# Two mixer layers: 22 of 62 convolution taps leave VectorE for ScalarE and GpSimd, small sums and weight splits come to it

## The chip, the cores and the metric

One core of a Trainium2 chip runs the kernel. The metric is the device time of one execution in microseconds. TensorE (PE) multiplies matrices, VectorE (DVE), ScalarE (ACT) and GpSimd (POOL) work on tiles of 128 partitions, and SyncE (SP) issues the loads. Each engine takes its instructions in a fixed order; semaphores hold one until the data and the buffers that it needs are there.

## The reference, cut to what matters

A first block of two layers, each `token_mixers` and `conv_ffn`, is followed by a second block of two layers that the change does not touch. The mixers of one layer (sequence 512, width 1024):

```python
def token_mixers(h, ...):
    proj = h @ w_in                                   # 512 x 1024 @ 1024 x D_IN, cut into 13 parts
    y_a = sc_b * depthwise_conv(sc_c * sc_h, w_sc_conv)          # 3 taps, 256 channels
    o_f = gla_scan(q, k, v, la_f, True)                          # linear attention, 4 heads, forward
    o_b = flip(gla_scan(flip(q), flip(k), flip(v), flip(la_b), False))   # and backward
    y_b = rms_norm(o_f + o_b, g_gla_head) * silu(gg)
    q_c = concat([qm[..., :64], apply_rope(qm[..., 64:])])       # 4 heads, 64 + 32 wide
    k_c = concat([kvm[..., :64], broadcast(apply_rope(kr))])
    y_c = blocked_attention(q_c, k_c, v_c, 96 ** -0.5)           # full softmax, 4 heads x 4 blocks
    u = depthwise_conv(a * sigmoid(gate), w_cfm_dw)              # 31 taps, 256 channels
    y_d = silu(layer_norm(u, g_cfm_ln, b_cfm_ln))
    y = concat([rms_norm(yb, gb) for yb, gb in zip((y_a, y_b, y_c, y_d), gains)])
    return y @ w_out
```

## The kernel before, in words

Activations lie feature-major, as tiles of 128 channels by 512 positions. A product of fp32 quality is made as three matmuls of reduced precision (`mm3`, lines 368 to 370): every operand is split into a rounded part `hi` (a ScalarE cast, line 374) and the rest `lo` (a subtraction, line 376). The weights stream from HBM in units of 128x1024 (`raw`) and are split on arrival. Most units have their `lo` made by VectorE; in the mixers `st.slow` (line 672) gives six units of a layer to GpSimd.

In `mixers_` four generators are written as if side by side, and `merge` (lines 237 to 249) lets that one go on which is furthest behind its share: `linear` (the linear attention), `mla` (softmax attention, 16 heads-by-blocks, each scores, softmax, transposes, values), `convolutions` (all the projections, then the two convolutions, then the first half of the output product) and `output` (the second half). This sets the program order. The tile framework then places each engine's instructions in a queue by its own simulated times (`schedule_with_timeline_sim=True`), keeping to what depends on what and to the buffers: a tile's name has a fixed number of buffers, and a new tile waits until the oldest one's last reader is done.

`convolutions` is the generator that the prediction follows. `projections` multiplies the last weights and makes the 3-tap branch `ya` (the last step is line 760). Then come `ya`'s squares (line 579), their sums over channels by 16 matmuls with one column (`feat_r`, line 562), and `ya`'s split into `g` for the output product (`put`, lines 890 and 891). The 31-tap convolution runs over two channel groups: 31 VectorE instructions each, all into `cacc` (lines 783 and 784). Its mean over channels comes from matmuls with ones (line 792), then follow the subtraction (795), squares, `feat_rsqrt`, gain, bias and the silu (801 to 806), `put`, and last `out_part` for the branches 0 and 3, whose first matmul is the first `L368 AP<-hi,g` of a layer's mixers. No output product stands ahead of it in TensorE's queue. The second half of the output product, the layer norm and the feed-forward part follow.

The lane `C` has four buffers named `Cw` of 128x512, shared by the projections' temporaries, `ya`, the squares and the tanh of the branch. `rsqrt` of up to 4 columns is a VectorE scale and a GpSimd power (lines 383 and 384). `feat_rsqrt` builds a diagonal matrix by VectorE (line 573) for each of 4 blocks and multiplies it by ones. The linear attention's running sums (lines 956 to 968) and the head mask (line 1008) are GpSimd's, and so are the 4 copies of the turned keys (line 1082). Each head's query is turned by three VectorE instructions of 32 partitions (lines 1073 to 1075).

Of the kernel before, what the change touches and what calls it, by code (L numbers as in the profile page):

```python
# [11 lines left out]
F32 = mybir.dt.float32  # L12
# [9 lines left out]
S = 512  # L22
# [12 lines left out]
SLOTS = 96  # L35

# [32 lines left out]
def layout(i):  # L69
# [11 lines left out]
    for l in range(2):  # L81
# [18 lines left out]
        q = []  # L100
        for h in range(4):
            r = rng(96 * h + 64, 32)
            q += rng(96 * h, 64) + r + r[16:] + r[:16]
# [156 lines left out]
class Lane:  # L260
# [23 lines left out]

    def d(self):
        return self.tile((128, 128), F32, "d", 2)


class Net:
# [351 lines left out]
    def block1_consts(self):  # L641
        self.gmask = self.blk.tile([128, 8, 128], U8, name="gmask")
        self.trig = self.blk.tile([128, S], F32, name="trig1")
        self.hmask = self.const("hmask", 256, self.blk)
# [5 lines left out]
    def mixers_(self, l, x):  # L650
# [7 lines left out]
        LN = Lane(self, "N", w=3)  # L658
# [13 lines left out]
        st.slow = (2, *range(6, 20, 3))  # L672
# [23 lines left out]
        with self.tc.issue_after(last.ins):  # L696
            if l == 0:
                raw = self.rawp.tile([128, 1024], F32, tag="raw", name=self.nm("raw"))
                nc.sync.dma_start(raw, self.A["gmask"])
                nc.gpsimd.tensor_copy(self.gmask.rearrange("p a b -> p (a b)"), raw)  # L700
                self.angles(M, "pos", 0, 1, 2, self.trig)
            tmp = M.w()
            ve.tensor_tensor(out=tmp[64:96], in0=kr[96:128], in1=self.trig[96:128], op=OP.mult)
            ve.tensor_tensor(out=kr[64:96], in0=kr[64:96], in1=self.trig[64:96], op=OP.mult)
            ve.tensor_tensor(out=kr[64:96], in0=kr[64:96], in1=tmp[64:96], op=OP.add)
# [65 lines left out]
        def convolutions():  # L771
# [122 lines left out]
    def gla_scores(self, L, q, k, dec):  # L894
# [41 lines left out]
        while m < 128:  # L936
# [19 lines left out]
            po.tensor_tensor(out=nf[:, :, 1], in0=fp[:, :, 1], in1=bc(ftl), op=OP.add)  # L956
            ac.copy(nf[:, :, 0], fp[:, :, 0])
            po.tensor_tensor(out=nb[:, :, 0], in0=bs[:, :, 0], in1=bc(btr), op=OP.add)
            ac.copy(nb[:, :, 1], bs[:, :, 1])
            if m == 1:  # L960
                po.tensor_copy(ns[:, :, 0], ftr)
                po.memset(ns[:, :, 1], 0.0)
                po.tensor_copy(np_[:, :, 1], btl)
                po.memset(np_[:, :, 0], 0.0)
            else:
                po.tensor_tensor(out=ns[:, :, 0], in0=fs[:, :, 0], in1=bc(ftr), op=OP.add)
                ac.copy(ns[:, :, 1], fs[:, :, 1])
                po.tensor_tensor(out=np_[:, :, 1], in0=bp[:, :, 1], in1=bc(btl), op=OP.add)
                ac.copy(np_[:, :, 0], bp[:, :, 0])
# [18 lines left out]
    def gla_states(self, L, inter, ends, gv):  # L988
# [4 lines left out]
        for d, order in enumerate(((0, 1, 2), (3, 2, 1))):  # L993
# [51 lines left out]
    def mla(self, L, wm, cq, ckv, kr, g_q, g_kv, attended):  # L1045
# [20 lines left out]
        def queries(h):  # L1066
            ps = L.P()
            for k in range(2):
                o = (2 * h + k) * 128
                nc.tensor.matmul(ps, wm[:, 0, o:o + 128], cq[k], start=k == 0, stop=k == 1)  # L1070
            ac.copy(Q[0:64, h], ps[0:64])
            tmp = L.w()
            ve.tensor_tensor(out=Q[64:96, h], in0=ps[64:96], in1=T[64:96], op=OP.mult)
            ve.tensor_tensor(out=tmp[64:96], in0=ps[96:128], in1=T[96:128], op=OP.mult)
            ve.tensor_tensor(out=Q[64:96, h], in0=Q[64:96, h], in1=tmp[64:96], op=OP.add)

        def keys(h):
            ps = L.P()
            nc.tensor.matmul(ps, wm[:, 1, h * 64:h * 64 + 128], ckv, start=True, stop=True)
            for j in range(2):  # L1080
                ac.copy(K[0:64, h + j], ps[64 * j:64 * j + 64])
                nc.gpsimd.tensor_copy(K[64:96, h + j], kr[64:96])
# [4 lines left out]
        for h in range(4):  # L1087
            queries(h)
            yield 1.7
# [969 lines left out]
```

## Time and profile before

| | |
|---|---|
| median of 3 runs | 3015.38 us (3015.05 to 3016.5) |
| the profiled execution, its own time | 3014.35 us |
| its span | 3012.6 us |
| busy in the span: PE / DVE / ACT / POOL | 95% / 72% / 48% / 15% |
| DVE instructions, POOL instructions | 3477, 443 |

The profiled execution lies 1.0 us under the median. A row of the profile gives line, engine, operation, names written and read (buffer numbers left out), shape and count, then busy time and the mean of one. An entry in brackets at the end of a timeline's row is the idle time of that engine before it and what ended it. Times of the timeline run from the span's start. "L784" is line 784 of the kernel before; the changed kernel's lines stand 3 to 4 lower up to line 600 and 10 to 20 higher from line 784 on.

### The profile page before, as it was taken

Reading aid. Unit: us, or ns where it says so; the run is one execution under the profiler, and the core shown is the slowest. Engines: PE = TensorE matmul, PEld = TensorE weight load, DVE = VectorE, ACT = ScalarE, POOL = GpSimd, SP = SyncE. Lnnn points to the kernel's source line nnn. Section 1 sums busy time; section 2 is a strip of 40 time slices with the busy share of each in tenths; the row PEclk is TensorE's granted clock in tenths of the full one; section 3 lists DMA queues with packets and bytes.
Section 4 is the critical chain, followed back from the end, with each engine's and each line's share of the span. In section 5 each row is a group of like instructions: output and inputs, shape, how many; then the busy total and the mean of one; then the engine's idle time right before and its main releaser. Section 6 shows DMA issues by size and latency. Waiting matters only on the chain.

```text
span 3012.6 us, 38089 instructions
## 1 busy us (share of the span) xinstructions
PE 2869.8 (95%) x14030; PEld 2250.3 (75%) x14030; DVE 2174.2 (72%) x3477; ACT 1434.1 (48%) x2214; POOL 456.2 (15%) x443
## 2 busy tenths in 40 slices
PE   7999999999999999999999998999799999979995
PEld 6777888888678888878777775776587877857773
DVE  6998655666968555687965467999678764579996
ACT  4444432324444333345444325887345444248883
POOL 3412000013111000012001021110311010022103
PEclk9999999999999999999999998999799999989998
DMA  5121332342213322352222377995631322669983
GB/s 191 35 106 49 99 98 92 99 143 70 64 54 95 98 98 98 106 170 89 78 88 84 105 264 266 379 389 223 230 109 60 95 88 80 245 224 374 384 321 135
DMA packets 128655, 457.35 MB, mean 152 GB/s; under 512 B 15761, under 2 KB 16977, under 8 KB 127057
## 3 DMA queue, kind: packets, MB, share of 16 engines
q1 hardware_dynamic: 117840, 425.50, 40.2%
q0 software_dynamic: 7168, 16.79, 1.8%
q10 hardware_dynamic: 3456, 12.58, 1.0%
q8 instruction: 112, 1.84, 0.2%
q14 instruction: 79, 0.64, 0.1%
HBM read 429.12 MB, written 27.26 MB: 151 GB/s over the span
## 4 chain that ended last, share of the span: by engine, by line
PE 64%; DVE 7%; ACT 2%; DMA 2%; issue 1%; POOL 1%; POOLq 0%; SPq 0%; DVEq 0%; ACTq 0%; another core or an unknown queue 0%
PE AP L368 12%; PE AP L369 12%; PE AP L370 12%; PE HP L368 4%; PE HP L369 4%; PE HP L370 4%; PE YP L369 2%; PE YP L370 2%; PE YP L368 2%; PE BP L369 1%; PE BP L370 1%; PE BP L368 1%; DVE cacc L784 1%; DVE lo L376 1%; PE O L1569 1%
## 5 line engine op out<-in xcount | busy, mean ns | idle before, releaser
L368 PE MATMUL AP<-g,hi 128*128 128x512 f32 (+1 forms) x1888 | 728.2, 387 | 25.3 <-ACT wide L445 7.4
L369 PE MATMUL AP<-g,hi 128*128 128x512 f32 (+1 forms) x1888 | 721.9, 383 | 8.2 <-DVE g L376 8.2
L370 PE MATMUL AP<-g,lo 128*128 128x512 f32 (+1 forms) x1888 | 723.0, 383 | 0.0
L376 DVE TENSOR_TENSOR lo<-raw,hi 128x1024 fp32r<-128x1024 f32 x322 | 409.6, 1274 | 371.4 <-ACT hi L374 362.2
L374 ACT CAST hi<-raw 128x1024 fp32r<-128x1024 f32 x334 | 350.1, 1051 | 581.9 <-PE AP L369 386.4
L368 PEld LDWEIGHTS AP<-g,hi 128*128 128x128 f32 x1888 | 360.3, 191 | 97.2 <-ACT wide L445 7.6
L369 PEld LDWEIGHTS AP<-g,hi 128*128 128x128 f32 x1888 | 360.4, 191 | 75.6 <-DVE g L376 9.2
L370 PEld LDWEIGHTS AP<-g,lo 128*128 128x128 f32 x1888 | 360.5, 191 | 67.5 <-issue 2.6
L376 DVE TENSOR_TENSOR lo<-g,hi 128x1024 fp32r<-128x1024 f32 x204 | 238.9, 1217 | 23.3 <-ACT hi L374 22.9
L376 DVE TENSOR_TENSOR lo<-wide,hi 128x1024 fp32r<-128x1024 f32 x188 | 221.9, 1225 | 40.7 <-ACT hi L374 40.5
L374 ACT CAST hi<-g 128x1024 fp32r<-128x1024 f32 x204 | 206.9, 1049 | 50.0 <-PE AP L370 32.5
L374 ACT CAST hi<-wide 128x1024 fp32r<-128x1024 f32 x188 | 190.6, 1048 | 47.8 <-DMA wide<-in_wmoed 26.8
L369 PE MATMUL HP<-lo,Txt 128*96 128x512 f32 x512 | 203.3, 397 | 0.8 <-DVE lo L376 0.6
L368 PE MATMUL HP<-hi,Txt 128*96 128x512 f32 x512 | 200.9, 400 | 1.1 <-ACT Txt L374 1.1
L370 PE MATMUL HP<-hi,Txt 128*96 128x512 f32 x512 | 202.0, 394 | 0.0
L368 PE MATMUL AP<-hi,g 128*128 128x512 f32 x416 | 171.4, 416 | 0.3 <-DVE g L886 0.3
L370 PE MATMUL AP<-hi,g 128*128 128x512 f32 x416 | 164.2, 397 | 0.2 <-DVE g L891 0.2
L369 PE MATMUL AP<-lo,g 128*128 128x512 f32 x416 | 163.0, 393 | 0.0
L368 PE MATMUL BP<-hi,g 128*128 128x512 f32 x352 | 136.8, 390 | 0.0
L369 PE MATMUL BP<-lo,g 128*128 128x512 f32 x352 | 136.6, 389 | 0.0
L370 PE MATMUL BP<-hi,g 128*128 128x512 f32 x352 | 134.1, 389 | 0.0
L369 PEld LDWEIGHTS HP<-lo,Txt 128*96 128x96 f32 x512 | 83.0, 162 | 39.8 <-DVE lo L376 4.1
(490 smaller groups left out, 4934.8 us busy)
## 6 DMA issues: line engine op xcount, KB each, us to landing
wide<-in_wmoeu SPq DMA_DIRECT2D x64, 1024.0 KB, 8.6
g<-in_wmoeu SPq DMA_DIRECT2D x64, 1024.0 KB, 8.6
raw<-in_wup SPq DMA_DIRECT2D x88, 512.0 KB, 3.5
g<-in_wmoed SPq DMA_DIRECT2D x34, 1024.0 KB, 9.1
wide<-in_wmoed SPq DMA_DIRECT2D x30, 1024.0 KB, 9.7
raw<-in_xwin SPq DMA_DIRECT2D x50, 512.0 KB, 3.7
raw<-in_xgate SPq DMA_DIRECT2D x48, 512.0 KB, 3.6
raw<-in_wdown SPq DMA_DIRECT2D x44, 512.0 KB, 3.5
```

The source lines that it names most:

```text
L368: mm(ps, a[0], b[0], start=start, stop=False)
L369: mm(ps, a[0], b[1], start=False, stop=False)
L370: mm(ps, a[1], b[0], start=False, stop=stop)
L374: self.nc.scalar.copy(hi, src)
L376: (engine or self.nc.vector).tensor_tensor(out=lo, in0=src, in1=hi.bitcast(F32), op=OP.subtract)
L784: ve.scalar_tensor_tensor(acc, ubs[c][:, j:j + S], w_dw[:, 31 * c + j:31 * c + j + 1], acc, op0=OP.mult, op1=OP.add)
L1569: nc.tensor.matmul(O[j][64 * b:64 * b + 64, t * 128:(t + 1) * 128], v[:, s, c:c + 64], PT[i - 1 + b][:, s, :], start=s == 0, stop=s == t, ...
```

## The change

Seven edits, all in the mixers. (1) `feat_rsqrt` multiplies the column `r`, broadcast as the left operand, by the identity; the diagonals and the lane's `d` are gone. (2) The linear attention's running sums and the head mask go from GpSimd to VectorE, its two plain copies to ScalarE. (3) All weight units have their `lo` made by VectorE. (4) Of each channel group's 31 taps 20 stay on VectorE (`MAIN_TAPS`). The other 11 are products by ScalarE; the first goes to a new tile `side` (one buffer), the others to `Cw` tiles, and GpSimd adds these to `side`. At the end VectorE adds `side` to `cacc`. (5) The query weights' columns are laid out anew, so that all four heads' turned parts come out together: 3 VectorE instructions of 128 partitions and 8 ScalarE copies in place of 12 VectorE instructions and 4 copies. The table `trig` is copied to all partitions by 8 DMAs of SyncE, once. (6) The turned keys are copied by ScalarE. (7) The layer norm's lane has two buffers, before three.

```diff
-            d = L.d()
-            nc.vector.tensor_scalar(d, self.ident, r[:, t:t + 1], None, op0=OP.mult)
-            nc.tensor.matmul(R[:, t * 128:(t + 1) * 128], self.ones, d, start=True, stop=True)
+            nc.tensor.matmul(R[:, t * 128:(t + 1) * 128], r[:, t:t + 1].to_broadcast([128, 128]), self.ident,
+                             start=True, stop=True)
...
-        LN = Lane(self, "N", w=3)
+        LN = Lane(self, "N", w=2)
...
-        st.slow = (2, *range(6, 20, 3))
...
-                self.angles(M, "pos", 0, 1, 2, self.trig)
+                trig = M.w()
+                self.angles(M, "pos", 0, 1, 2, trig)
+
+                for i in range(2):
+                    for h in range(4):
+                        nc.sync.dma_start(out=self.trig[32 * h:32 * h + 32, i], in_=trig[64 + 32 * i:96 + 32 * i])
...
-                acc = self.pp.tile([128, S], F32, tag="cacc", bufs=2, name=self.nm("cacc"))
-                ve.tensor_scalar(acc, ubs[c][:, 0:S], w_dw[:, 31 * c:31 * c + 1], None, op0=OP.mult)
-                for j in range(1, 31):
-                    ve.scalar_tensor_tensor(acc, ubs[c][:, j:j + S], w_dw[:, 31 * c + j:31 * c + j + 1], acc,
-                                            op0=OP.mult, op1=OP.add)
+                acc, side = (self.pp.tile([128, S], F32, tag=n, bufs=b, name=self.nm(n))
+                             for n, b in (("cacc", 2), ("side", 1)))
+                tap = lambda j: (ubs[c][:, j:j + S], w_dw[:, 31 * c + j:31 * c + j + 1])
+                ve.tensor_scalar(acc, *tap(0), None, op0=OP.mult)
+                apart = list(range(MAIN_TAPS, 31))
+                for j in range(1, MAIN_TAPS):
+                    a, w = tap(j)
+                    ve.scalar_tensor_tensor(acc, a, w, acc, op0=OP.mult, op1=OP.add)
+                    if j % 3 != 2 and apart:
+                        i = apart.pop(0)
+                        a, w = tap(i)
+                        term = side if i == MAIN_TAPS else C.w()
+                        ac.activation(term, a, AF.Copy, scale=w)
+                        if i > MAIN_TAPS:
+                            nc.gpsimd.tensor_tensor(out=side, in0=side, in1=term, op=OP.add)
                     if j % 10 == 0:
                         yield 0.5
+                assert not apart
+                ve.tensor_tensor(out=acc, in0=acc, in1=side, op=OP.add)
                 u.append(acc)
...
-            po.tensor_tensor(out=nf[:, :, 1], in0=fp[:, :, 1], in1=bc(ftl), op=OP.add)
+            ve.tensor_tensor(out=nf[:, :, 1], in0=fp[:, :, 1], in1=bc(ftl), op=OP.add)
...
-                po.tensor_copy(ns[:, :, 0], ftr)
+                ac.copy(ns[:, :, 0], ftr)
...
-                    po.tensor_tensor(out=s, in0=s, in1=self.hmask, op=OP.mult)
+                    ve.tensor_tensor(out=s, in0=s, in1=self.hmask, op=OP.mult)
...
-            ac.copy(Q[0:64, h], ps[0:64])
-            tmp = L.w()
-            ve.tensor_tensor(out=Q[64:96, h], in0=ps[64:96], in1=T[64:96], op=OP.mult)
-            ve.tensor_tensor(out=tmp[64:96], in0=ps[96:128], in1=T[96:128], op=OP.mult)
-            ve.tensor_tensor(out=Q[64:96, h], in0=Q[64:96, h], in1=tmp[64:96], op=OP.add)
+            if i < 2:
+                for j in range(2):
+                    ac.copy(Q[0:64, 2 * i + j], ps[64 * j:64 * j + 64])
+                return
+            turned.append(L.w())
+            ve.tensor_tensor(out=turned[-1], in0=ps, in1=T[:, i - 2], op=OP.mult)
+            if i == 3:
+                ve.tensor_tensor(out=turned[0], in0=turned[0], in1=turned[1], op=OP.add)
+                for h in range(4):
+                    ac.copy(Q[64:96, h], turned[0][32 * h:32 * h + 32])
...
-                nc.gpsimd.tensor_copy(K[64:96, h + j], kr[64:96])
+                ac.copy(K[64:96, h + j], kr[64:96])
```

How the queues stand now, in layer 0 (layer 1 has the same pattern). First ScalarE around the end of the projections. In the kernel before, L579 on `Cw` squares `ya`, L579 on `cacc` squares the finished convolution, L890 is `ya`'s put, L1107, L1040 and L998 are the attentions':

```order
L579 ACTIVATE Cw_1613<-Cw_1565 128x512
L1107 COPY Mw_1592<-T_1587 128x512
L1040 ACTIVATE Mw_1596,Ms_290_1601<-MP_1594,Ms_289_1599 128x512
L998 COPY Gw_1501<-GP_1497 128x384
L579 ACTIVATE Cw_1707<-cacc_1632 128x512
L579 ACTIVATE Cw_1710<-cacc_1668 128x512
L1107 COPY Mw_1781<-T_1776 128x512
L890 ACTIVATE g_1610<-Cw_1352,vec_215 128x512
L890 ACTIVATE g_1610<-Cw_1565,vec_215 128x512
```

Now L575 squares `ya`, L903 is its put, and L794 is a tap's product, read from the padded input `pad`:

```order
L575 ACTIVATE Cw_1599<-Cw_1551 128x512
L1127 COPY Mw_1578<-T_1573 128x512
L1053 ACTIVATE Mw_1582,Ms_281_1587<-MP_1580,Ms_280_1585 128x512
L903 ACTIVATE g_1596<-Cw_1338,vec_215 128x512
L903 ACTIVATE g_1596<-Cw_1551,vec_215 128x512
L794 ACTIVATE Cw_1625<-pad_760,vec_215 128x512
L794 ACTIVATE Cw_1629<-pad_760,vec_215 128x512
L794 ACTIVATE Cw_1634<-pad_760,vec_215 128x512
L1011 COPY Gw_1560<-GP_1556 128x384
L1127 COPY Mw_1869<-T_1864 128x512
L1053 ACTIVATE Mw_1873,Ms_356_1878<-MP_1871,Ms_355_1876 128x512
L794 ACTIVATE Cw_1638<-pad_760,vec_215 128x512
```

The products stand behind `ya`'s squares and puts; where the convolution's squares stood, the second to fourth of its products stand now. Of 22 products one, the first of the first channel group, stands earlier (it goes to `side`); the other 21 are spread over the 45 rows that follow.

Second GpSimd, from the last running sums on, in the kernel before (L384 is the power of a `rsqrt`, of the convolutions' lane C, the softmax attention's M or the linear attention's G; L1008 the head mask):

```order
L966 TENSOR_TENSOR g_594<-g_594,g_477 128x4x64
L968 TENSOR_TENSOR g_594<-g_594,g_477 128x4x64
L384 TENSOR_TENSOR Cs_298_1625<-Cs_297_1624,mhalf 128x4
L1008 TENSOR_TENSOR g_1496<-g_1496,c_hmask 128x256
L384 TENSOR_TENSOR Cs_309_1722<-Cs_308_1721,mhalf 128x4
L1008 TENSOR_TENSOR g_1496<-g_1496,c_hmask 128x256 x2
L384 TENSOR_TENSOR Ms_366_1932<-Ms_365_1931,mhalf 128x1
L1008 TENSOR_TENSOR g_1496<-g_1496,c_hmask 128x256
L384 TENSOR_TENSOR Gs_351_1866<-Gs_350_1865,mhalf 128x4
L384 TENSOR_TENSOR Gs_355_1874<-Gs_354_1873,mhalf 128x1
```

And now the same place, with L796 the additions of products to `side` and L381 the powers:

```order
L796 TENSOR_TENSOR side_1619<-side_1619,Cw_1625 128x512
L796 TENSOR_TENSOR side_1619<-side_1619,Cw_1629 128x512
L381 TENSOR_TENSOR Cs_289_1611<-Cs_288_1610,mhalf 128x4
L796 TENSOR_TENSOR side_1619<-side_1619,Cw_1634 128x512
L796 TENSOR_TENSOR side_1619<-side_1619,Cw_1638 128x512
L381 TENSOR_TENSOR Ms_375_1954<-Ms_374_1953,mhalf 128x1
L796 TENSOR_TENSOR side_1619<-side_1619,Cw_1643 128x512
L796 TENSOR_TENSOR side_1619<-side_1619,Cw_1647 128x512
L796 TENSOR_TENSOR side_1619<-side_1619,Cw_1652 128x512
L381 TENSOR_TENSOR Gs_360_1888<-Gs_359_1887,mhalf 128x4
```

Twenty additions and ten powers stand in 30 rows, one addition behind the other on the same tile, and a power waits behind the additions ahead of it.

Third VectorE, from the sums of `ya`'s squares to the subtraction of the convolution's mean. Before (L383 scales the sums of `ya`'s squares, L795 subtracts the mean):

```order
L1042 RECIPROCAL Ms_291_1603<-Ms_290_1601 128x1
L1100 TENSOR_SCALAR Mw_1596<-Mw_1596,Ms_291_1603 128x512
L383 TENSOR_SCALAR Cs_297_1624<-AP_1615 128x4
L795 SCALAR_TENSOR_TENSOR cacc_1632<-AP_1703,cacc_1632 128x512
L795 SCALAR_TENSOR_TENSOR cacc_1668<-AP_1703,cacc_1668 128x512
```

Now (L800 adds `side`, L808 subtracts the mean, L1041 to L1045 and L380 are the linear attention's output, L814 the gain):

```order
L380 TENSOR_SCALAR Gs_433_2141<-Gs_408_2084 128x4
L1045 TENSOR_TENSOR Gv_602<-Gv_602,Gs_434_2142 128x256
L380 TENSOR_SCALAR Gs_437_2149<-Gs_436_2147 128x1
L800 TENSOR_TENSOR cacc_1672<-cacc_1672,side_1673 128x512
L808 SCALAR_TENSOR_TENSOR cacc_1618<-AP_1730,cacc_1618 128x512
L808 SCALAR_TENSOR_TENSOR cacc_1672<-AP_1730,cacc_1672 128x512
L380 TENSOR_SCALAR Cs_319_1748<-AP_1739 128x4
L814 SCALAR_TENSOR_TENSOR cacc_1618<-cacc_1618,vec_215,AP_1752 128x512
```

The subtraction stood right behind row L383 of `ya`; now 50 rows lie between, the last of them the second group's L800, behind the linear attention's whole output. TensorE's first output product stands behind all of this in both kernels: before it, TensorE has small matmuls of the two attentions alone, now including 12 transposes of the softmax attention (L1105 before) and the linear attention's last products, 8 of them L1023 by the trace's count, which stood behind it before.

## Rows read from the trace of the kernel before

**Rows 1.** The page's chain that ended last, shares of the span by engine

```profile
PE 64%; DVE 7%; ACT 2%; DMA 2%; issue 1%; POOL 1%; POOLq 0%; SPq 0%; DVEq 0%; ACTq 0%; another core or an unknown queue 0%
```

**Rows 2.** Windows: stretch; length, busy us (instructions) per engine, PEclk, DMA share, GB/s

```profile
60.00:196.00 136.00, 127.94 (x676) 95.84 (x674) 129.16 (x190) 57.61 (x122) 39.49 (x42) 0.96 0.18 59
740.00:829.00 89.00, 86.08 (x421) 63.01 (x420) 87.71 (x137) 33.38 (x72) 13.16 (x15) 0.98 0.19 60
120.00:140.00 20.00, 20.00 (x95) 13.54 (x94) 19.95 (x30) 9.28 (x20) 4.54 (x4) 1.00 0.09 27
820.00:840.00 20.00, 20.00 (x124) 15.15 (x123) 14.94 (x27) 5.85 (x10) 1.19 (x1) 0.89 0.51 192
```

**Rows 3.** Chain of waits in 655 to 965 us: share by line

```profile
by line: DVE cacc L784 12.4%; PE AP L368 9.6%; PE AP L370 8.9%; PE AP L369 8.9%; issue 4.7%; PE MP L1095 3.2%; PE O L1118 3.1%; DVE g L923 3.0%; DVE lo L376 3.0%; PE GP L915 2.7%; PE T L1105 2.1%; PE AP L562 1.7%; PE GP L1023 1.3%; PE AP L7
```

**Rows 4.** VectorE's groups in 60 to 196 us: busy us, mean ns of one, idle before

```profile
L784 DVE SCALAR_TENSOR_TENSOR cacc<-pad,vec,cacc 128x512 f32<-128x512 f32 x60 | 47.8, 821 | 0.3
L376 DVE TENSOR_TENSOR lo<-raw,hi 128x1024 fp32r<-128x1024 f32 x12 | 14.9, 1252 | 0.2 <-ACT hi L374 0.2
L1074 DVE TENSOR_TENSOR Mw<-MP,trig 32x512 f32<-32x512 f32 x4 | 2.8, 696 | 0.1
L573 DVE TENSOR_SCALAR Md<-c_ident,Ms 128x128 f32<-128x128 f32 x8 | 3.3, 432 | 0.0
```

**Rows 5.** Timeline of VectorE and GpSimd: start us, us, engine, line

```profile
124.89 0.41 DVE L721 TENSOR_TENSOR Gv<-Gv,Gv 128x256 f32<-128x256 f32 x1
128.45 4.04 DVE L784 SCALAR_TENSOR_TENSOR cacc<-pad,vec,cacc 128x512 f32<-128x512 f32 x6
132.75 2.82 DVE L784 SCALAR_TENSOR_TENSOR cacc<-pad,vec,cacc 128x512 f32<-128x512 f32 x1
132.68 2.35 POOL L376 TENSOR_TENSOR lo<-raw,hi 128x1024 fp32r<-128x1024 f32 x1 [13.11 <-ACT hi L374]
```

**Rows 6.** Timeline of layer 0's mixers, 192 to 221 us

```profile
192.86 0.39 PE L370 MATMUL AP<-g,lo 128*128 128x512 f32 x1
198.28 1.62 PE L562 MATMUL AP<-ones,Cw 128*128 128x1 f32 x14
200.12 1.02 PE L792 MATMUL AP<-cacc,ones 128*128 128x512 f32 x2
220.64 0.47 PE L368 MATMUL AP<-hi,g 128*128 128x512 f32 x1
```

**Rows 7.** Timeline of layer 1's mixers, 829 to 866 us

```profile
829.05 0.39 PE L370 MATMUL AP<-g,lo 128*128 128x512 f32 x1
835.72 0.59 PE L562 MATMUL AP<-ones,Cw 128*128 128x1 f32 x2
838.23 3.78 PE L792 MATMUL AP<-cacc,ones 128*128 128x512 f32 x4
865.83 0.48 PE L368 MATMUL AP<-hi,g 128*128 128x512 f32 x1
```

**Rows 8.** GpSimd's groups over the whole span; the last row gives min/median/max ns

```profile
L1348 POOL TENSOR_TENSOR g<-g,Bw 128x512 f32<-128x512 f32 x16 | 23.5, 1466 | 112.4 <-DVE Bw L1346 76.5 <-DVE Is L1042 26.5 <-issue 9.4
L1520 POOL TENSOR_TENSOR Bw<-Bw 128x511 f32<-128x511 f32 x8 | 8.3, 1034 | 0.0
L384 POOL TENSOR_TENSOR Gs<-Gs,mhalf 128x4 f32<-128x4 f32 x8 | 8.6, 1080 | 13.6 <-DVE Gs L383 13.6
L384 POOL TENSOR_TENSOR Gs<-Gs,mhalf 128x1 f32<-128x1 f32 x8 | 4.4, 552 | 18.0 <-DVE Gs L383 18.0
L1348 POOL TENSOR_TENSOR g<-g,Bw x16: 1277/1294/2209, 1583.6 to 2528.0; 128x512 f32<-128x512 f32 x16
```

**Rows 9.** Line 579 on ScalarE, ns min/median/max, first and last start

```profile
L579 ACT ACTIVATE Cw<-Cw x4: 626/628/630, 187.3 to 830.3; 128x512 f32<-128x512 f32 x4
```

**Rows 10.** TensorE's groups in 220.6 to 296.7 us

```profile
L1105 PE MATMUL T<-c_ident,Mw 128*128 128x128 f32 x40 | 6.2, 273 | 0.0
L1023 PE MATMUL GP<-Gv,g 128*128 128x64 f32 x8 | 1.0, 268 | 0.0
```

More of the change, by code (lines that the diff above doesn't have):

```diff
@@ L35 @@
 SLOTS = 96
+MAIN_TAPS = 20
 def fm_unit(w, cols):
@@ L99, in layout @@
         uq = f("w_mla_uq")[l]
[L100 to L103, printed above, removed]
+        turns = [rng(96 * h + 64, 32) for h in range(4)]
+        q = [i for h in range(4) for i in rng(96 * h, 64)]
+        q += [i for r in turns for i in r] + [i for r in turns for i in r[16:] + r[:16]]
         uq = uq.reshape(2, 128, 384)[:, :, q].reshape(2, 128, 4, 128).transpose(1, 2, 0, 3).reshape(128, 1024)
@@ L283, in s @@
         return self.tile(shape, dt, *(("s16", 12) if n <= 16 else ("s64", 4)))
-    def d(self):
-        return self.tile((128, 128), F32, "d", 2)
 class Net:
@@ L642, in block1_consts @@
         self.gmask = self.blk.tile([128, 8, 128], U8, name="gmask")
-        self.trig = self.blk.tile([128, S], F32, name="trig1")
+        self.trig = self.blk.tile([128, 2, S], F32, name="trig1")
         self.hmask = self.const("hmask", 256, self.blk)
@@ L700, in mixers_ @@
                 nc.gpsimd.tensor_copy(self.gmask.rearrange("p a b -> p (a b)"), raw)
-                self.angles(M, "pos", 0, 1, 2, self.trig)
+                trig = M.w()
[3 more added lines that the diff above has]
+                        nc.sync.dma_start(out=self.trig[32 * h:32 * h + 32, i], in_=trig[64 + 32 * i:96 + 32 * i])
             tmp = M.w()
-            ve.tensor_tensor(out=tmp[64:96], in0=kr[96:128], in1=self.trig[96:128], op=OP.mult)
-            ve.tensor_tensor(out=kr[64:96], in0=kr[64:96], in1=self.trig[64:96], op=OP.mult)
+            ve.tensor_tensor(out=tmp[64:96], in0=kr[96:128], in1=self.trig[96:128, 1], op=OP.mult)
+            ve.tensor_tensor(out=kr[64:96], in0=kr[64:96], in1=self.trig[64:96, 0], op=OP.mult)
             ve.tensor_tensor(out=kr[64:96], in0=kr[64:96], in1=tmp[64:96], op=OP.add)
@@ L955, in gla_scores @@
             btl, btr = bs[:, :, 0, 0:1], bs[:, :, 1, 0:1]
-            po.tensor_tensor(out=nf[:, :, 1], in0=fp[:, :, 1], in1=bc(ftl), op=OP.add)
+            ve.tensor_tensor(out=nf[:, :, 1], in0=fp[:, :, 1], in1=bc(ftl), op=OP.add)
             ac.copy(nf[:, :, 0], fp[:, :, 0])
-            po.tensor_tensor(out=nb[:, :, 0], in0=bs[:, :, 0], in1=bc(btr), op=OP.add)
+            ve.tensor_tensor(out=nb[:, :, 0], in0=bs[:, :, 0], in1=bc(btr), op=OP.add)
             ac.copy(nb[:, :, 1], bs[:, :, 1])
             if m == 1:
-                po.tensor_copy(ns[:, :, 0], ftr)
+                ac.copy(ns[:, :, 0], ftr)
                 po.memset(ns[:, :, 1], 0.0)
-                po.tensor_copy(np_[:, :, 1], btl)
+                ac.copy(np_[:, :, 1], btl)
                 po.memset(np_[:, :, 0], 0.0)
             else:
-                po.tensor_tensor(out=ns[:, :, 0], in0=fs[:, :, 0], in1=bc(ftr), op=OP.add)
+                ve.tensor_tensor(out=ns[:, :, 0], in0=fs[:, :, 0], in1=bc(ftr), op=OP.add)
                 ac.copy(ns[:, :, 1], fs[:, :, 1])
-                po.tensor_tensor(out=np_[:, :, 1], in0=bp[:, :, 1], in1=bc(btl), op=OP.add)
+                ve.tensor_tensor(out=np_[:, :, 1], in0=bp[:, :, 1], in1=bc(btl), op=OP.add)
                 ac.copy(np_[:, :, 0], bp[:, :, 0])
@@ L1064, in mla, with queries @@
         yield 1
[L1066 removed]
+        def queries(i):
             ps = L.P()
             for k in range(2):
[L1069 removed]
+                o = (2 * i + k) * 128
                 nc.tensor.matmul(ps, wm[:, 0, o:o + 128], cq[k], start=k == 0, stop=k == 1)
[L1071 to L1075 removed]
+            if i < 2:
[8 more added lines that the diff above has]
+                    ac.copy(Q[64:96, h], turned[0][32 * h:32 * h + 32])
         def keys(h):
@@ L1086, in mla @@
             yield 1
-        for h in range(4):
-            queries(h)
+        turned = []
+        for i in (2, 3, 0, 1):
+            queries(i)
             yield 1.7
```

## The prediction, made before the changed kernel had run

> **What bounds the kernel now.** I read the chain that ended last first: TensorE has 64% of it, VectorE 7%, GpSimd 1% [rows 1]. TensorE bounds the kernel as a whole, so an edit of other engines is worth what it takes from or adds to TensorE's waiting. Next the windows of the two mixers: from 60 to 196 us VectorE is busy 129.16 of 136 us, from 740 to 829 us 87.71 of 89 [rows 2]. TensorE is busy nearly as long, 127.94 and 86.08, and where VectorE is full it is too (120 to 140 us). The chain over layer 1 names the convolution's taps with 12.4%, more than any other line [rows 3]. So in these two stretches VectorE's queue, the taps above all, sets when the last projection can run; GpSimd has 39.49 and 13.16 us of work there and ScalarE under half.
>
> Third, what stands behind these stretches. The last projection ends at 193.25 us in layer 0 and 829.44 us in layer 1; the first output product starts at 220.64 and 865.83 us [rows 6, 7]. These waits of 27.4 and 36.4 us hold the branch's norm and the small matmuls of both attentions. The work behind them waits for that first output product, since it stands behind it in TensorE's queue. A change of this wait is therefore a change of the time, except for work that is pulled into it.
>
> **What the change does on VectorE before the wait.** Per layer, with the durations of this profile:
> - 22 taps less. Six taps in a row with GpSimd idle take 4.04 us, 0.673 each [rows 5]; the mean in the stretch is 0.821 [rows 4]. At 0.673: -14.8 us.
> - 26 sums of 128x256 more. The nearest row is a 128x256 addition at 0.41 us [rows 5]: +10.7. With broadcast operands they can't be much below; a 512-wide tap's 0.673 is the upper end, +17.5.
> - 6 splits at 1.252 [rows 4]: +7.5.
> - The turns: 12 at 0.69 (L1073 and L1075 are near the row of L1074) go, 3 of 128x512 at about 0.75 come: -6.0. The 11 diagonals ahead of the wait, at 0.43 [rows 4]: some -4.
> - Together -14.8 + 10.7 + 7.5 - 6.0 - 4 = -6.6 us.
> - Less blocking: a tap that ran beside a GpSimd split of 2.35 us took 2.82 us [rows 5]. GpSimd's splits and sums in the stretch go, so the 38 taps that are left should fall from 0.821 towards 0.673: -5.6, and the two-input multiplications of the linear attention some -2.
>
> VectorE is thus done about 14 us earlier per layer. TensorE can't take all of it: by its busy time it idles only 8.06 us in the first stretch and 2.92 in the second [rows 2], though busy times of pipelined matmuls hide part of the idling. I take -9 and -7, bounds -5.5 (the mean of the two idle times) and -14 each.
>
> ScalarE gets 22 products of about 0.63 us [rows 9], 8 key and 8 query copies and two copies of sums; it has room (57.61 of 136 us, [rows 2]). Eight transfers for the table, once, and LN's smaller lane I cost at nothing: they lie beside projections that wait for VectorE; if the table's transfers come late the turned keys' copies hold ScalarE's queue, up to 3 us, once.
>
> **What it does in the wait.** By the order of ScalarE's queue, all but one of the 22 products stand behind `ya`'s squares and puts, because their tiles are the lane's four `Cw`, which hold the projections' temporaries, `ya` and its squares until then. So the additions can't start before the column sums over `ya`'s squares have read them. That is 199.90 us in layer 0 (198.28 + 1.62) and 836.31 in layer 1 (835.72 + 0.59), 6.65 and 6.87 us behind the last projection [rows 6, 7]. From there the chain to the first output product is:
> - first product, 0.63 [rows 9];
> - 20 GpSimd additions of two 128x512 tiles, one behind the other on `side`. The trace has no such line in the mixers; the same shape elsewhere has a median of 1.294, least 1.277, mean 1.466, and a 511-wide addition with one source tile 1.034 [rows 8]. I take 1.294, the median of the same shape: 25.9; bounds 20.7 and 29.3;
> - ten powers that stand between the additions, five 128x4 and five 128x1, at 1.080 and 0.552 [rows 8]: 8.2;
> - waiting of GpSimd in its order: `side` has one buffer, so the second group's first product waits for VectorE's L800, and four powers wait for VectorE's and ScalarE's steps of the linear attention. Products themselves come at 0.63 and don't limit. I take 4, bounds 0 and 8;
> - the second group's L800, 0.7;
> - the branch's norm, from the second mean's matmuls to the first output product. Before it took 20.5 us in layer 0 (200.12 to 220.64) and 27.6 in layer 1 (838.23 to 865.83) [rows 6, 7], beside both attentions on VectorE. After the change most heads are through by then: I take 18, bounds 14 and 23.
>
> Sum: 6.7 + 0.6 + 25.9 + 8.2 + 4 + 0.7 + 18 = 64.1 us in place of 27.4 and 36.4: +36.7 and +27.7, together +64.4. In the kernel before nothing of the first five terms was in the wait: VectorE had done all taps when the column sums ran.
>
> What TensorE does meanwhile counts back: 12 transposes at 6.2/40 and 8 value products for 1.0 us [rows 10] are pulled ahead, 2.9 per layer, -6 for both. The rest of the attention can't come: its heads stand behind output products in the queue. Of the clock: from 820 to 840 us, where TensorE had gaps, the granted clock was 0.89, against 1.00 in a full stretch [rows 2]. Longer gaps cost a little more of this; 1 us per layer, +2, bounds 0 and 8.
>
> All together: +64.4 - 9 - 7 - 6 + 2 = +44.4. The profiled execution's 3014.35 becomes 3058.8; it lies 1.0 under the median, so I say 3059. That is slower: VectorE is unloaded where it bounds, but the convolution's second half moves from an engine that was done at the last projection to one that can only start there.
>
> **A rule that speaks on this.** The row of the tap at 2.82 us beside GpSimd's 2.35 us shows VectorE held for the length of a GpSimd instruction [rows 5]. The Trainium skill's page "SBUF — State Buffer", section "SBUF: two separate sides", says that the two share a port pair which is locked for a whole instruction when VectorE has two SBUF inputs; the trace agrees, since 2.35 + 0.67 would be 3.02. By the rule GpSimd's 20 additions would in turn be held by VectorE's puts and gains, which is rival 3 below.
>
> **The rivals.**
> 1. *VectorE's relief decides, and it is faster.* If the products came early, beside the projections, as the diff alone would let one think, the additions would be done by the time the taps are, and the wait would stay at 27.4 and 36.4 us. Then only the relief counts: -16 us, 2999. It decides if the first output product starts within some 42 us of the last projection in the mean of both layers (31.9 as before, plus half of the 16 + 6 - 2 that comes back). For it: VectorE's busy 98% from 740 to 829 us [rows 2]. Against it: the sum without any waiting and with the norm at 14 is 6.7 + 0.6 + 20.7 + 8.2 + 0.7 + 14 = 50.9. Chance 0.11. The Trainium skill's page "Perfetto Trace Analysis", section "Optimizing Scalar/DVE Operations", says that with VectorE saturated some work may well go to ScalarE or even GpSimd, though between VectorE and GpSimd it might not help; the full VectorE windows meet its condition.
> 2. *The two cancel.* Additions at 1.034 without waits give the 50.9 us just worked out: +38.0 for both waits; with the relief at its bound of 14 each and the 6 pulled ahead, +4: 3019. For it: GpSimd is alone on long stretches of the wait. Against: no 128x512 addition of two tiles was under 1.277 [rows 8]. Chance 0.06.
> 3. *Blocking both ways, much slower.* Additions at 1.466, GpSimd waiting 8, the norm as before at 20.5 to 27.6 (24): 6.7 + 0.6 + 29.3 + 8.2 + 8 + 0.7 + 24 = 77.5; +91 for both, -11 of relief, -6, +8 of clock: +82, 3097. For it: taps at 2.82 [rows 5]. Against: in the wait VectorE's work is short. Chance 0.09.
>
> **How the numbers follow.** My forecast has 0.74 with its own range 3035 to 3085: additions and waits at their nearer bounds and the relief between -11 and -24. The range for 8 in 10 reaches to the cancelling case, leaves out most of rival 1 and half of rival 3: 3018 to 3092. This kernel's measurement can't tell changes within 0.2%, 6 us, from none. Rival 1 is the chance of faster, 0.11; rival 2 is the chance of no change, 0.06; the rest, 0.83, is slower.
>
> **What will show it.** GpSimd has a line of 40 additions at about 1.3 us, in layer 0 from about 190 to 235 us; between them hardly a gap. TensorE's windows show idling and a clock under 1.00 in the 40 us behind the last projection, which itself comes some 9 and 7 us earlier; the first output product follows it by about 64 us in both layers. The taps' mean is near 0.68, VectorE's busy share in the wait is low. I am wrong if the first output product comes within 42 us, if additions take 1.0 us or less, if the projections end no earlier, or if products appear on ScalarE among the projections.

## The result and the profile after

The changed kernel takes 3082.68 us (median of 4 runs, 3079.21 to 3086.52) where the kernel before took 3015.94 beside it: the ratio is 1.0224, with a 95% interval from 1.0211 to 1.0237. It is 66.7 us slower. The forecast was 3059, that is +44, with a range from 3018 to 3092.

The profiled execution of the changed kernel has a span of 3078.8 us, 66.2 more than before. Cut at the end of the last projection, the first output product and the first matmul of the feed-forward part, the two traces compare like this (us). The first output product is the first `AP<-hi,g` behind the last projection; the `AP<-hi,g` that stand earlier in a layer's mixers, from 106.22 us on in layer 0 before, are the value projections:

| stretch | before | after | change | forecast |
|---|---|---|---|---|
| to layer 0's last projection | 193.25 | 193.15 | -0.1 | -9 |
| wait, layer 0 | 27.4 | 63.3 | +35.9 | +36.7 |
| first output product to the end of the mixers, layer 0 | 76.1 | 78.1 | +2.1 | -2 |
| from there to layer 1's last projection | 532.8 | 529.0 | -3.7 | -7 |
| wait, layer 1 | 36.4 | 63.4 | +27.0 | +27.7 |
| first output product to the end of the mixers, layer 1 | 74.0 | 74.4 | +0.4 | -2 |
| the rest of the span | 2072.8 | 2077.5 | +4.6 | 0 |

The waits come out as forecast. This is TensorE in layer 0 of the changed kernel, to be held against [rows 6]:

```profile
192.76 0.39 PE L367 MATMUL AP<-g,lo 128*128 128x512 f32 x1
198.24 1.62 PE L559 MATMUL AP<-ones,Cw 128*128 128x1 f32 x14
239.61 2.07 PE L805 MATMUL AP<-cacc,ones 128*128 128x512 f32 x2 [11.70 <-DVE cacc L800]
256.45 0.77 PE L365 MATMUL AP<-hi,g 128*128 128x512 f32 x1
```

The second mean's matmuls (L805) stood idle for 11.70 us until VectorE's L800, and L800 waits for the last addition. GpSimd's queue from its first addition on, in the same layer (between the third and the fourth row it goes on in the same way):

```profile
200.54 3.61 POOL L796 TENSOR_TENSOR side<-side,Cw 128x512 f32<-128x512 f32 x2 [33.58 <-ACT Cw L794]
204.11 1.20 POOL L381 TENSOR_TENSOR Cs<-Cs,mhalf 128x4 f32<-128x4 f32 x1
205.29 2.67 POOL L796 TENSOR_TENSOR side<-side,Cw 128x512 f32<-128x512 f32 x2
...
229.33 1.26 POOL L796 TENSOR_TENSOR side<-side,Cw 128x512 f32<-128x512 f32 x1
231.68 0.56 POOL L381 TENSOR_TENSOR Gs<-Gs,mhalf 128x1 f32<-128x1 f32 x1 [1.09 <-DVE Gs L380]
232.21 6.63 POOL L796 TENSOR_TENSOR side<-side,Cw 128x512 f32<-128x512 f32 x5
```

It had been idle for 33.58 us and starts when the first product lands, 0.7 us behind the column sums (199.86). That product had stood in ScalarE's queue right behind `ya`'s puts, and then waited for those column sums (L559) to give its tile free:

```profile
198.08 1.32 ACT L903 ACTIVATE g<-Cw,vec 128x512 fp32r<-128x512 f32 x2
199.74 1.95 ACT L794 ACTIVATE Cw<-pad,vec 128x512 f32<-128x512 f32 x3 [0.33 <-PE AP L559]
```

One addition follows the other, with the powers between, until 238.83. And the additions in both layers, with the engines that wait for them (min/median/max in ns, then idle us and times):

```profile
L796 POOL TENSOR_TENSOR side<-side,Cw x40: 1255/1264/2197, 200.5 to 908.1; 128x512 f32<-128x512 f32 x40
...
  DVE cacc L800: 14.5, 2
  ACT Cw L794: 11.2, 13
```

The last row says that ScalarE's products wait for the additions to give a tile free, 13 times; once GpSimd has started, it waits for a product only twice, 1.4 us in both layers.

What did not come is the relief. Windows as in [rows 2] (the second moved by 38 us, as the end of layer 0's mixers is; its last 3.4 us lie in the wait), and then three from the wait on:

```profile
60.00:196.00 136.00, 128.22 (x692) 97.95 (x691) 109.24 (x183) 66.19 (x136) 3.01 (x4) 0.96 0.21 62
778.00:867.00 89.00, 89.00 (x471) 65.09 (x470) 73.45 (x122) 38.34 (x78) 0.13 (x2) 1.00 0.19 60
220.00:240.00 20.00, 4.04 (x15) 2.09 (x15) 7.64 (x16) 7.80 (x18) 16.17 (x15) 0.59 0.00 0
240.00:260.00 20.00, 11.50 (x39) 8.88 (x38) 8.91 (x19) 7.67 (x16) 1.02 (x1) 0.50 0.00 1
260.00:280.00 20.00, 20.00 (x95) 14.75 (x96) 9.34 (x21) 5.54 (x12) 1.55 (x2) 0.80 0.00 1
```

VectorE is busy 109.24 us in place of 129.16 in layer 0 and 73.45 in place of 87.71 in layer 1, about the 14 us less that were forecast or more, and the taps have a mean of 748 ns in place of 821:

```profile
L789 DVE SCALAR_TENSOR_TENSOR cacc<-pad,vec,cacc 128x512 f32<-128x512 f32 x38 | 27.7, 748 | 0.2
```

The projections end at the same time in layer 0 and 3.7 us earlier in layer 1, where TensorE is now busy all of the 89 us. The third figure from the end is the granted clock: 0.50 of full speed from 240 to 260 us, the lower of the two levels, 1.2 GHz, and still 0.80 on the mean of the 20 us behind, though TensorE is busy all of them.

### The profile page after: what moved, and what is told of

Its sections match the earlier page's. It is cut to its first block, busy times and chain, and to the rows that moved or that the text cites. A ratio compares the mean times of both kernels' runs of the same rounds, so it can differ in the third digit from the quotient of the medians.

```text
span 3078.8 us, 38125 instructions
## 1 busy us (share of the span) xinstructions
PE 2885.8 (94%) x14030; PEld 2264.3 (74%) x14030; DVE 2154.2 (70%) x3467; ACT 1473.7 (48%) x2278; POOL 419.5 (14%) x399
## 4 chain that ended last, share of the span: by engine, by line
PE 86%; DVE 6%; ACT 2%; POOL 2%; issue 2%; DMA 2%; SPq 0%; POOLq 0%; DVEq 0%; another core or an unknown queue 0%; ACTq 0%
PE AP L365 17%; PE AP L366 16%; PE AP L367 16%; PE HP L365 4%; PE HP L366 4%; PE HP L367 4%; PE BP L366 3%; PE BP L367 3%; PE BP L365 3%; PE YP L366 2%; PE YP L367 2%; PE YP L365 2%; DVE lo L373 1%; PE GP L928 1%; POOL side L796 1%
## 5 line engine op out<-in xcount | busy, mean ns | idle before, releaser
L373 DVE TENSOR_TENSOR lo<-raw,hi 128x1024 fp32r<-128x1024 f32 x334 | 422.6, 1267 | 384.1 <-ACT hi L371 372.7
```

The lines of the kernel that those rows point to most:

```text
L373: (engine or self.nc.vector).tensor_tensor(out=lo, in0=src, in1=hi.bitcast(F32), op=OP.subtract)
```

## The experiments

Theory S: the loss is the chain of additions that can't start before `ya`'s tiles are free and that runs one by one behind the projections. Rival Q: the other edits lose it, in the queues at 70 to 100 us. Rival L: it is GpSimd and VectorE blocking each other. Each time stands beside runs of the kernel before on the same chip.

**The taps alone.** The kernel before with this edit, and two buffers in the norm's lane:

```diff
-        LN = Lane(self, "N", w=3)
+        LN = Lane(self, "N", w=2)
...
+                        ac.activation(term, a, AF.Copy, scale=w)
+                        if i > MAIN_TAPS:
+                            nc.gpsimd.tensor_tensor(out=side, in0=side, in1=term, op=OP.add)
...
```

> The kernel before with the divided taps alone (and two buffers in the layer norm's lane, for room); sums, splits, turns and diagonals as before. Theory S (the serial GpSimd additions behind the projections are the loss): the wait from the last projection to the first output product is 60 to 68 us in both layers, as in the changed kernel's 63.3, and the time is 3070 to 3085. Rival Q (the loss comes from the other edits, through ScalarE's and VectorE's queues at 70 to 100 us): the time is under 3040.

Measured: 3094.61 us, ratio 1.0263 (1.0246 to 1.0280); the waits are 66.9 and 66.1 us. The taps alone lose more than the whole change, so the rest of the change gains 0.4% beside them. Q falls. The time is above the stated range.

**All but the taps.** The changed kernel with the old loop of 31 taps:

```diff
-                for j in range(1, MAIN_TAPS):
-                    a, w = tap(j)
...
+                for j in range(1, 31):
+                    ve.scalar_tensor_tensor(acc, ubs[c][:, j:j + S], w_dw[:, 31 * c + j:31 * c + j + 1], acc,
+                                            op0=OP.mult, op1=OP.add)
```

> The changed kernel with all 31 taps of a channel group on VectorE again; every other edit stays. Theory S: the waits fall back to 25 to 38 us, and the time lies between 3005 and 3025, since VectorE has some 8 us more work per layer ahead of the last projection than before, less 5 to 8 of blocking by GpSimd. Rival Q: 3045 or more.

Measured: 3025.65, ratio 1.0039 (1.0024 to 1.0053), just above the expected range. The waits are 21.4 and 22.7 us, shorter than before and than S expected. But from the first output product to the mixers' end it is now 92.2 and 89.8 us (before 76.1 and 74.0). Near its end TensorE waits for the softmax of the last heads:

```profile
289.56 0.43 PE L1126 MATMUL O<-Mw,Mv 128*64 128x128 f32 x2 [0.67 <-ACT Mw L1115]
294.70 0.66 PE L1113 MATMUL T<-c_ident,Mw 128*128 128x128 f32 x2 [4.71 <-DVE Mw L1108]
```

In this run 9 heads' maxima start behind the first output product, in the kernel before 8 and 7; in layer 0 TensorE has 131 matmuls in the wait and 444 behind it, before 177 and 405. So a shorter wait isn't all gain: work that was done in it stands behind it. The other edits lose 11 us here and gain 12 beside the divided taps: their worth hangs on the order around them.

**26 taps on VectorE.**

```diff
-MAIN_TAPS = 20
+MAIN_TAPS = 26
```

> The changed kernel with 26 taps of a group on VectorE in place of 20: 8 additions per layer on GpSimd in place of 20. Theory S: each wait falls by 12 x 1.34 = 16 us to about 47, the last projection comes 0 to 8 us later, the time is 3048 to 3060. Rival N (the wait is set by the powers and the norm between them, the additions lie beside them): the wait falls by under 8 us and the time stays over 3066.

Measured: 3051.68, ratio 1.0122 (1.0105 to 1.0139); the waits are 47.3 and 47.4 us. Here is the first output product, 47.3 us behind the end of the last projection at 194.30:

```profile
241.62 0.77 PE L365 MATMUL AP<-hi,g 128*128 128x512 f32 x1
```

Twelve additions less shorten the wait by 16.0 us, 1.33 for each: the additions are the wait, one for one. N falls.

**The same taps, written earlier.** The generator's loop over the taps is called behind the value projections:

```diff
             ready.add("values")
+            yield from taps()
```

> The changed kernel with the taps of both groups written right behind the value projections, ahead of the 3-tap branch, so that the products find free Cw tiles; the same instructions. Theory S: the additions are done before the last projection, the waits are 25 to 38 us, and the time is 3000 to 3025. Rival L (a GpSimd addition blocks VectorE's two-input instructions for its length): the waits fall too, but the taps' mean goes from 0.75 to over 1.0 us, the last projection comes 8 us or more later in each layer, and the time is over 3025.

Measured: 3052.37, ratio 1.0117 (1.0097 to 1.0138). The waits are 28.0 and 25.2 us: S is right on the wait and wrong on the time. The last projection comes at 210.51 us, 17 later, and in layer 1 it is 544.5 us behind layer 0's mixers, in place of 529.0. Up to 210.51 us TensorE idles 34.5 us, in place of 25.1 up to its last projection in the changed kernel, and its clock is 0.93 in place of 0.97. Six taps and five additions beside each other, VectorE and then GpSimd (start, us):

```profile
116.44 10.21 DVE L737 SCALAR_TENSOR_TENSOR cacc<-pad,vec,cacc 128x512 f32<-128x512 f32 x6
```

```profile
117.73 8.37 POOL L744 TENSOR_TENSOR side<-side,Cw 128x512 f32<-128x512 f32 x5
```

A tap takes 1.70 us here, with GpSimd idle 0.673 [rows 5]; an addition 1.67, in the changed kernel's wait 1.26 (the median). In layer 0 the taps' mean is 1003 ns, over both layers the additions' is 1586:

```profile
L737 DVE SCALAR_TENSOR_TENSOR cacc<-pad,vec,cacc 128x512 f32<-128x512 f32 x38 | 37.1, 1003 | 0.2
```

```profile
L744 POOL TENSOR_TENSOR side<-side,Cw 128x512 f32<-128x512 f32 x40 | 63.4, 1586 | 37.7 <-ACT Cw L742 26.2 <-ACT side L742 8.8
```

The slower taps, 38 x (1.003 - 0.748), are 9.7 of the 17 us; the rest is not taken apart here. So L is right too, in the other place: behind the projections the additions are the wait, beside the taps they block them. The Trainium skill's page "SBUF — State Buffer", section "SBUF: two separate sides", says that a VectorE instruction with two SBUF inputs and a GpSimd instruction that reads SBUF exclude each other for their whole length; the rows agree in direction, not in full, as the pair takes 1.70 us and one behind the other would take 0.673 + 1.26 = 1.93.

**Single edits taken back, from the run without the divided taps (3025.65).** First the heads turned one by one as before:

```diff
-        for i in (2, 3, 0, 1):
-            queries(i)
+        for h in range(4):
+            queries(h)
...
```

> The run with all taps back on VectorE (3025.65 us), and the queries turned head by head as before, with the old table. Theory T (in layer 0 the table's way through ScalarE and SyncE makes the gap of 6.3 us at 73 us, which eats VectorE's relief): the gap falls to the 4 us of before or less, layer 0's last projection ends by 189 us, and the time falls by 3 to 6 us, to about 3021. Rival O (the gap is the running sums' way through VectorE's and ScalarE's queues): the gap stays, VectorE has 6 us more per layer, and the time is 3025 to 3035.

Measured: 3016.09, ratio 0.9999 (0.9990 to 1.0008). The gap at 73 us stays, so the table is not its cause:

```profile
78.64 1.71 PE L912 MATMUL GP<-Gw,Gw 32*128 32x128 f32 x10 [6.17 <-ACT g L917]
```

Layer 0's last projection ends at 188.56 all the same, so neither theory is right as it stood. Up to there TensorE idles as much as before, 24.6 us (25.0 before), but has 900 matmuls in place of 914: less work stands ahead. Layer 1 is 11.5 us shorter than before, while layer 0 is 16 us longer: behind its last projection it takes 124 us in place of 103, and from its first output product on TensorE has 437 matmuls in place of 405, at a clock of 0.88 in place of 1.00.

Then the sums on GpSimd, and, apart from it, the splits:

```diff
-            ve.tensor_tensor(out=nf[:, :, 1], in0=fp[:, :, 1], in1=bc(ftl), op=OP.add)
+            po.tensor_tensor(out=nf[:, :, 1], in0=fp[:, :, 1], in1=bc(ftl), op=OP.add)
...
```

> The run with all taps back on VectorE, and the linear attention's sums, copies and head mask on GpSimd again. Theory P (VectorE's queue bounds the stretch, and 10.7 us of sums per layer cost more there than the blocking by GpSimd): the last projection comes 3 to 6 us earlier in each layer, the time is 3010 to 3018. Rival B (blocking by GpSimd costs as much as the sums do): taps go from 0.75 to 0.80 us or more, the projections end no earlier, and the time is 3023 to 3030. By theory O of the run before, the gap at 73 us in layer 0 shrinks here.

```diff
         st = self.stream(f"win{l}")
+        st.slow = (2, *range(6, 20, 3))
```

> The run with all taps back on VectorE, and six weight splits per layer on GpSimd again. By the blocking (a tap beside a split of 2.35 us took 2.82) it is a wash: VectorE gives up 7.5 us of splits and gets 6 splits of about 2.4 us, each blocking most of its length: the time is within 5 us of 3025. If VectorE's queue were relieved by it in full, 3015 or less.

Measured: 3029.34 (1.0045, 1.0031 to 1.0059) and 3025.84 (1.0033, 1.0021 to 1.0045), both beside 3025.65 (1.0039). For the sums P falls and B holds on the time and the projections: the last one comes 2 us later in layer 0 and 3 in layer 1. But the taps go only from 0.75 to 0.77 and 0.78 us, less than B wanted, and the gap at 73 us in layer 0 does not shrink as was expected: TensorE now waits 2.50, 3.62 and 3.30 us between 72 and 86 us, 9.4 in all in place of 7.8. The splits are the expected wash, with taps of 0.79 us.

**The diagonals alone.** The kernel before with this:

```diff
-            d = L.d()
-            nc.vector.tensor_scalar(d, self.ident, r[:, t:t + 1], None, op0=OP.mult)
-            nc.tensor.matmul(R[:, t * 128:(t + 1) * 128], self.ones, d, start=True, stop=True)
+            nc.tensor.matmul(R[:, t * 128:(t + 1) * 128], r[:, t:t + 1].to_broadcast([128, 128]), self.ident,
+                             start=True, stop=True)
```

> The kernel before with the diagonals alone gone: VectorE has 12 instructions of 0.28 to 0.43 us per layer less, some 4 us, and TensorE takes the broadcast column as left operand. If TensorE minds the broadcast operand, the matmuls of line 569 are slower than the old 574. Expected: -2 to -6 us against the kernel before, 3009 to 3013; same if the small instructions lay in VectorE's idle time.

Measured: 3042.61, ratio 1.0086 (1.0072 to 1.0100). That is 27 us the other way, for VectorE work taken off. The matmul itself is not slower: 16 of them take 2.1 us, with the diagonal 16 took 3.1. But the scheduler placed the heads anew: in layer 0 TensorE has 134 matmuls in the wait and 445 behind it, before 177 and 405. In both layers a gap like that of the second run stands before the last ones (layer 1's):

```profile
945.91 0.43 PE L1117 MATMUL O<-Mw,Mv 128*64 128x128 f32 x2 [0.99 <-ACT Mw L1106]
950.83 1.09 PE L1104 MATMUL T<-c_ident,Mw 128*128 128x128 f32 x4 [4.48 <-DVE Mw L1099]
```

and the clock is down behind it (two windows of 10 us, then two of the kernel before at the same place of its layer 1):

```profile
940.00:950.00 10.00, 5.35 (x38) 3.77 (x36) 8.62 (x19) 4.80 (x10) 2.97 (x3) 0.87 0.11 40
950.00:960.00 10.00, 7.97 (x32) 6.32 (x33) 1.69 (x6) 1.84 (x5) 1.93 (x2) 0.50 0.04 14
```

```profile
920.00:930.00 10.00, 10.00 (x58) 7.98 (x54) 9.11 (x19) 4.33 (x8) 3.40 (x4) 1.00 0.00 0
930.00:940.00 10.00, 8.87 (x52) 6.32 (x51) 9.82 (x18) 6.73 (x10) 4.70 (x5) 1.00 0.19 54
```

**Layer 1 alone.** The edits of the run that gave 3016.09, made where this is true:

```diff
+        self.second = l > 0
+        self.sums = ve if self.second else nc.gpsimd
...
+        if l == 0:
+            st.slow = (2, *range(6, 20, 3))
...
```

> The kernel before in layer 0; in layer 1 the edits of the run that gave 3016.09 us (sums, copies and head mask on VectorE and ScalarE, all splits on VectorE, no diagonals, keys copied by ScalarE, two buffers in the norm's lane; taps and turns as before). In that run layer 1 was 11.5 us shorter from the end of layer 0's mixers to the end of its own (526.9 + 104.7 against 532.8 + 110.4) and layer 0 longer by 16. Theory V (VectorE's relief is worth that much where the queue order behind it is kept): layer 0 as before within 1 us, layer 1 shorter by 6 to 13, 3002 to 3010 us. Rival C (the 11.5 us hang on the order in which the heads happen to stand): layer 1 within 4 us of before, 3011 to 3020.

Measured: 3010.17, ratio 0.9978 (0.9968 to 0.9988). From the end of layer 0's mixers to the end of its own layer 1 takes 633.7 us where it took 643.1, -9.5; V holds, though the median lies just above its range and layer 0 is 1.8 us longer. This is the lowest ratio here, by a little over what can be told from no change; the next run's 0.9981 can't be told from it.

**The heads' place in the queue.** The run that gave 3016.09, with this:

```diff
-        merge((linear(), 31), (self.mla(M, wm, cq, ckv, kr, g_q, g_kv, attended), 29), (convolutions(), 112),
+        merge((linear(), 31), (self.mla(M, wm, cq, ckv, kr, g_q, g_kv, attended), 38), (convolutions(), 112),
```

> The run that gave 3016.09 us, with the softmax attention's share in the merge of the four generators raised from 29 to 38, so that five heads, before three, stand ahead of the last projection in TensorE's queue; no other edit. Theory H (behind the projections the rest of the attention sets the time, some 6.8 us a head): the last projection comes 3 to 6 us later in both layers, the stretch from there to the mixers' end is shorter by 8 to 20 us, the time is 2995 to 3010. If the output products and the clock set it, the time is 3014 to 3025.

Measured: 3012.34, ratio 0.9981 (0.9971 to 0.9990). Layer 0 takes 101 us behind its last projection in place of 124, as H says, but that projection comes 6.8 us later. Layer 1 loses 8.4 us: its projection comes 6.9 us later behind layer 0's mixers, and from there to the mixers' end it takes 106.2 in place of 104.8. The median lies above H's range.

The same edit on the kernel before:

> The kernel before with the same share of 38 and nothing else, as the control of the run before: by theory H it gains too, 3003 to 3012; VectorE is full ahead of the last projection here, so the heads delay it by more, 5 to 10 us per layer, and the time may come out at 3010 to 3020.

Measured: 3021.38, ratio 1.0014 (1.0006 to 1.0023). The heads delay the projections by 3 us in layer 0 and 6 in layer 1, and behind them 3.5 and 5.7 come back: layer 1's mixers end at 940.40 us in place of 939.79. H's gain is missing; the time is within what counts as no change, and above both ranges.

The same edit with the diagonals gone:

> The kernel before without the diagonals, with the softmax attention's share at 38. The removal alone gave 3042.6 us, with a gap of 4.6 us before the last heads in both layers and the clock at 0.50 to 0.87 behind it. Theory H (that loss is the place of the last heads in TensorE's queue, which the scheduler chose anew, not the matmul with a broadcast column): with the heads earlier the gap goes and the time is 3008 to 3022. If the broadcast column itself costs, it stays over 3035.

Measured: 3031.10, ratio 1.0043 (1.0030 to 1.0057), between the two theories. The stretches behind the first output product fall from 92 and 89 to 75 and 76 us, as H says, but the projections of layer 0 end 9.6 us later; 14 of the 27 us stay. Of the 9.6 us, 9.1 are TensorE's own busy time: 977 matmuls stand ahead of the last projection in place of 916, at a clock of 0.94 in place of 0.96. So the heads' place explains the longer end, not all of the loss, and where the other half of it comes from is open.

## Why the prediction was right, and where it was short

- *The wait* was right in mechanism and in size: 63.3 and 63.4 us, forecast 64.1. From the first addition to the last it takes 38.3 us in both layers (200.54 to 238.83); the forecast's additions, powers and waiting were 25.9 + 8.2 + 4 = 38.1; in layer 0 they measure 26.7, 8.1 and 3.1. One addition has a median of 1.264 and a mean of 1.337, where 1.294 was taken from [rows 8]. A product takes 0.72 us, where 0.63 was taken from [rows 9]. The norm takes 16.8 us behind that, forecast 18. The run with 8 additions in place of 20 shows that they cause it, the run with the taps written earlier that their place behind `ya` does.
- *VectorE's relief* is the step that failed in size: "I take -9 and -7", and -0.1 and -3.7 came. That is 12.2 of the 22 us by which the traces' +66.2 goes beyond +44.4. VectorE did become free, by 20 us in layer 0 and some 14 in layer 1. But TensorE had only 8.06 and 2.92 us of idling to give back [rows 2]. The prediction had these numbers and went above them, since busy times might hide idling. They came nearer: in layer 1 the gain is about its 2.92 us, and TensorE is full there now. They are no hard bound, though: in the run with all but the taps the same stretch is 6.8 us shorter than before, as TensorE's idling falls from 6.95 to 4.51 us and its busy time from 525.80 to 521.45, at a clock of 1.00 in place of 0.99. In layer 0 the idling stays at 7.78 of 136 us. At 79 us TensorE now waits 6.16 us for ScalarE, and then for VectorE, in the scores of the linear attention; before, there was one gap of 3.98 us near this place. First the changed kernel's rows, then that of before:

```profile
79.38 2.56 PE L928 MATMUL GP<-Gw,Gw 32*128 32x128 f32 x16 [6.16 <-ACT g L933]
83.56 0.79 PE L928 MATMUL GP<-Gw,Gw 32*128 32x128 f32 x2 [1.62 <-DVE g L936]
```

```profile
74.13 0.50 PE L368 MATMUL AP<-g,hi 128*128 128x512 f32 x1 [3.98 <-ACT Mw L711]
```

  These gaps are not the whole account of layer 0. In the run with the taps alone the gap is 3.98 us as before, VectorE is busy 117.16 us in place of 129.16, and the last projection still ends at 193.61. Up to there TensorE idles 22.4 us in place of 25.0, but it is busy 171.2 in place of 168.2, with 927 matmuls in place of 914 and a clock of 0.96 in place of 0.97. The gap and the window of that run:

```profile
74.05 0.79 PE L369 MATMUL AP<-g,hi 128*128 128x512 f32 x1 [3.98 <-ACT Mw L712]
60.00:196.00 136.00, 130.36 (x682) 97.30 (x681) 117.16 (x169) 58.65 (x124) 38.84 (x42) 0.95 0.18 59
```

  Why a less busy VectorE gives TensorE next to nothing in layer 0 stays open.
- *The pulled work and the clock*, together -4, measured +2.5. The pulled matmuls are there: 28 and 22 fewer stand behind the first output product. But the output products start at half the clock, since the wait has put TensorE at 0.50, and stay there for some 11 us in layer 0 and 4 in layer 1, as the spacing of the matmuls shows (0.43 us, then 0.23). By that the clock cost some 5 and 2 us, an estimate. Its +2 was mis-sized, and its source misread: the prediction speaks of gaps from 820 to 840 us, but TensorE was busy all 20.00 us there, at 0.89 [rows 2]. The windows in which the clock is still low, first layer 0's, then layer 1's:

```profile
260.00:270.00 10.00, 10.00 (x47) 7.83 (x49) 2.60 (x7) 3.29 (x6) 1.01 (x1) 0.59 0.00 0
922.00:932.00 10.00, 5.50 (x30) 4.91 (x31) 7.20 (x17) 7.95 (x16) 0.10 (x1) 0.58 0.00 0
```

- *The rest of the span*, +4.6, was not in the forecast. Nothing is changed there; in the other runs the same stretch takes 2072 to 2077 us. Its cause is open.
- *The rivals.* "VectorE's relief decides" needed products among the projections; one of 22 stood there, as the order of the queue had shown. The run that put them there lost by rival 3's mechanism instead. The Trainium skill's page "Perfetto Trace Analysis", section "Optimizing Scalar/DVE Operations", warns that moving work between VectorE and GpSimd might not help; both placements of the additions agree in the outcome: against the run without the divided taps (1.0039) they give 1.0224 behind the projections and 1.0117 beside them. Behind the projections it is the chain that costs, though, and not blocking.
- *Diagonals, splits, sums* were costed one by one by VectorE's time, and that sum is no guide: the diagonals alone lose 27 us, the splits are a wash, the sums on VectorE gain at most 4, the new turns lose 10.

## What to carry to other kernels

Before work is moved to an idle engine, ask when its inputs and buffers allow it to start, and who waits for its end: 21 of 22 products came only behind the last projection, and 20 additions of 1.3 us became a wait for TensorE. Count a chain of accumulations on one tile as serial time. Where a scheduler sets the queues, an edit's price is read from the new order around the bounding engine, and an edit that suits one layer is worth trying there alone: here that gave 0.9978, hardly more than no change.

## What the runs showed of the hardware that was not expected

Taps on VectorE and additions on GpSimd that run beside each other both slow down, to 1.70 and 1.67 us from 0.673 and 1.26, so that a tap moved away saves VectorE 0.67 us and costs it 1.03 for each other tap that meets an addition. And a gap of 4.48 us on TensorE was followed by a granted clock of 0.50 over the next window of 10 us, where the kernel before had 1.00 at the same place of its layer: here a short wait near the end of a stage was paid again in slow matmuls.
